# Output projection of a hybrid encoder block: 20 of 32 contraction tiles by one Strassen level

## The chip, the core and the metric

One NeuronCore of a Trainium2 chip runs the whole block in one launch. The metric is the device time of that launch in microseconds (us), and a time is given as the median of several runs. TensorE (PE in the rows, PEld for its weight loads) multiplies, VectorE (DVE) and ScalarE (ACT) work on elements, GpSimd (POOL) and SyncE (SP) mostly start DMA transfers.

## What is computed

The input x is 512 tokens by 4096 channels in float32. One layer:

```
h = rmsnorm(x) * pre_norm
z = h @ w_in            # 9808 columns: q, c, qi, kix, wix, gate_a, pool_in, gate_b
ya = sparse_attention(q, c, qi, kix, wix) * silu(gate_a)      # 2048 channels
yb = multiscale_pool(pool_in) @ w_pool * scale * silu(gate_b) # 2048 channels
y = concat(ya, yb) @ w_out                                    # 4096 x 4096
out = x + rmsnorm(y) * post_norm
```

The change concerns the product with `w_out`: 512 tokens, contraction over 4096 channels, 4096 output columns.

## The kernel before

Every float32 product is made of three matmuls on halves of the numbers: `split` (lines 57 to 59) casts a tile to a rounded type on ACT (the high half, `hi`) and subtracts it from the original on DVE (the low half, `lo`); `mm3` (lines 70 to 74) adds high x high, high x low and low x high in PSUM. `staged` (lines 61 to 68) loads a 128 x 512 weight tile of 256 KB through SP's DMA queue and splits it; its three buffers `raw`, `hi`, `lo` have four places each, so weights can be prepared four tiles ahead.

The channels are cut into 32 tiles of 128 (`NK`), the tokens into 4 blocks of 128 (`NB`). A first stage normalises x and keeps the halves `xh`, `xl` of all 32 tiles in SBUF, in 32 buffers of the pool `big`. Then `group` (lines 235 to 245) makes 128 columns of z at a time: 8 weight tiles, 32 x 3 matmuls into one bank of PSUM, an evacuation, and between the weight tiles one step of a background queue `bg` (lines 247 to 268) that spreads attention and pooling over the groups. The gated results, 32 tiles of 128 channels x 512 tokens, go to a DRAM tensor `cat` (`put`, line 334). The last groups are those of the fourth pool group (`pool_group`, lines 349 to 395, with g = 3), each followed by a gate.

The output projection follows (lines 481 to 557). `reload` brings tiles of `cat` back, splits them, and keeps the halves `ch`, `cl` in the buffers that `xh` and `xl` had. `chunk(db, blocks)` makes 512 output columns for the given token blocks: for each of the 32 contraction tiles one weight tile of `wout` and 12 matmuls of 512 columns (6 for two blocks). Its result is squared and summed on ACT and multiplied by the gain on DVE (lines 504 to 509). The column blocks 0 to 4 (`NFULL` = 5) take all four token blocks at once; blocks 5 to 7 take token blocks 0 and 1 first, so that `finish((0, 1))` can write half of the output while blocks 5 to 7 run again for tokens 2 and 3, with their weights loaded a second time. `finish((2, 3))` comes at the end: 16 multiply-adds on DVE, each followed by a store.

The code is traced; a scheduler then orders each engine's instructions, and each engine executes its own list in that order.

Of the kernel before, what the change touches and what calls it, by code (L numbers as in the profile page):

```python
# [43 lines left out]
def block_kernel(ctx: ExitStack, tc: tile.TileContext, xT, x, gk, wc, wkw, wf, wuk, wuv, kvn,  # L44
                 ikg, ikb, wpool, pscale, wout, gpost, ident_in, invc_in, out):
# [288 lines left out]
    def put(e, src, scl, sg):  # L334
        V.scalar_tensor_tensor(sg, src, scl, sg, op0=ALU.mult, op1=ALU.mult)
        if e == NK - 1:
            split(sg, *[t[:, 1] for t in cat_tile(NK // 2 - 1)])
        else:
            nc.sync.dma_start(cat[e], sg)

    ct = {}

    def cat_tile(i):
        if i not in ct:
            ct[i] = (big.tile([P, 2, S], F32R, tag=f"h{i}", name=f"ch{i}"),
                     big.tile([P, 2, S], F32R, tag=f"l{i}", name=f"cl{i}"))
        return ct[i]

    def pool_group(pl, g):
# [36 lines left out]
        for d in range(4):  # L386
            yp = bank()
            bg.add(ymix(d, yp), 1)

            def evac(z, d=d, yp=yp):  # L390
# [229 lines left out]
```

## Time and profile before

| what | value |
| --- | --- |
| median of 3 runs | 2624.4 us (2623.66 to 2629.9) |
| span of the profiled execution (no other time is listed for it) | 2626.6 us |
| TensorE busy, matmuls | 2587.6 us (99%), 11768 |
| DVE busy, ACT busy, POOL busy | 1176.9 us (45%), 863.8 us (33%), 46.7 us (2%) |
| DMA, mean over the span | 119 GB/s |
| loads of `wout` | 352 of 256 KB |

Matmuls are pipelined: the duration in a row runs from a matmul's start to its modelled end and overlaps the next ones. What a matmul costs in a stream is the distance between two starts. Idle time of an engine that is not the bottleneck costs nothing by itself.

### The profile page before, as it was taken

The page shows a single profiled execution, that of the slowest core. Times are in us where ns is not written, and L with a number is a line of the kernel's source. Part 1 is how long each engine was busy: PE and PEld are TensorE (multiplying, and loading weights), DVE is VectorE, ACT ScalarE, POOL GpSimd, SP SyncE. Part 2 cuts the span into 40 slices and gives each one's busy share as a digit, 9 for nine tenths or more (in the row PEclk, how much of TensorE's full clock was granted, in tenths as well). Part 3 has the DMA queues.
Part 4 walks back from the last instruction along what each step waited for, and adds up shares of the span by engine and source line. Part 5 has one row for each costly group of instructions (what it writes and reads, how often), then busy time and mean ns, then how long its engine had stood idle before and what let it go on. Part 6 is the DMA issues. An engine that isn't in the chain of part 4 may idle for free.

```text
span 2626.6 us, 31765 instructions
## 1 busy us (share of the span) xinstructions
PE 2587.6 (99%) x11768; PEld 2147.4 (82%) x11768; DVE 1176.9 (45%) x2086; ACT 863.8 (33%) x1542; POOL 46.7 (2%) x36
## 2 busy tenths in 40 slices
PE   7999999999999999999999999999999999999997
PEld 5799888888888888888888888888888888888875
DVE  9465783344344444444344334344452222235655
ACT  5344322233333333333332222222342222235443
POOL 5100000000000000000000000000000000000000
PEclk9999999999999999999999999999999999999998
DMA  6334333333333333333333333333473333346786
GB/s 202 99 100 109 96 100 107 103 92 90 98 94 92 89 97 92 92 93 92 94 93 97 106 106 96 105 104 101 129 224 101 101 97 103 101 133 197 224 284 220
DMA packets 169068, 312.15 MB, mean 119 GB/s; under 512 B 19536, under 2 KB 19664, under 8 KB 168912
## 3 DMA queue, kind: packets, MB, share of 16 engines
q1 hardware_dynamic: 168912, 310.12, 40.5%
q8 instruction: 92, 1.51, 0.2%
q14 instruction: 64, 0.52, 0.1%
HBM read 293.53 MB, written 16.52 MB: 118 GB/s over the span
## 4 chain that ended last, share of the span: by engine, by line
PE 90%; DMA 2%; DVE 1%; ACT 0%; issue 0%; DVEq 0%; SPq 0%; ACTq 0%
PE ps_acc L72 21%; PE ps_acc L74 20%; PE ps_acc L73 20%; PE ps_w L73 9%; PE ps_w L74 9%; PE ps_w L72 9%; DMA raw<-in_wout 2%; PE ps_w L447 1%; PE ps_w L279 1%; DVE lo L59 0%; DVE xr L530 0%; DMA xr<-in_x 0%; ACT hi L58 0%; DMA out<-xr 0%; DVE yg L509 0%
## 5 line engine op out<-in xcount | busy, mean ns | idle before, releaser
L59 DVE TENSOR_TENSOR lo<-raw,hi 128x512 fp32r<-128x512 f32 x1008 | 698.7, 695 | 1216.7 <-ACT hi L58 1143.2
L58 ACT CAST hi<-raw 128x512 fp32r<-128x512 f32 x1008 | 626.2, 622 | 1548.4 <-PE ps_acc L73 929.1
L72 PE MATMUL ps_acc<-xh,hi 128*128 128x512 f32 (+1 forms) x2304 | 893.0, 388 | 0.0
L74 PE MATMUL ps_acc<-xh,lo 128*128 128x512 f32 (+1 forms) x2304 | 883.9, 384 | 0.0
L73 PE MATMUL ps_acc<-xl,hi 128*128 128x512 f32 (+1 forms) x2304 | 883.7, 384 | 0.0
L72 PEld LDWEIGHTS ps_acc<-xh,hi 128*128 128x128 f32 x2304 | 432.7, 188 | 81.5 <-issue 2.2
L74 PEld LDWEIGHTS ps_acc<-xh,lo 128*128 128x128 f32 x2304 | 432.4, 188 | 81.4 <-issue 0.2
L73 PEld LDWEIGHTS ps_acc<-xl,hi 128*128 128x128 f32 x2304 | 433.0, 188 | 76.3
L73 PE MATMUL ps_w<-lo,ch 128*128 128x512 f32 x864 | 338.3, 392 | 3.3 <-DVE lo L59 3.2
L72 PE MATMUL ps_w<-hi,ch 128*128 128x512 f32 x864 | 337.2, 390 | 1.8 <-ACT hi L58 1.8
L74 PE MATMUL ps_w<-hi,cl 128*128 128x512 f32 x864 | 336.9, 390 | 0.0
L73 PEld LDWEIGHTS ps_w<-lo,ch 128*128 128x128 f32 x864 | 162.6, 188 | 41.8 <-DVE lo L59 8.3
L72 PEld LDWEIGHTS ps_w<-hi,ch 128*128 128x128 f32 x864 | 162.5, 188 | 36.7 <-ACT hi L58 2.7
L74 PEld LDWEIGHTS ps_w<-hi,cl 128*128 128x128 f32 x864 | 162.6, 188 | 33.4
L73 PE MATMUL ps_w<-lo,xh 128*128 128x512 f32 x128 | 52.9, 414 | 9.6 <-DVE lo L59 9.6
L72 PE MATMUL ps_acc<-hi,ch 128*128 128x512 f32 x160 | 62.2, 389 | 0.0
L73 PE MATMUL ps_acc<-lo,ch 128*128 128x512 f32 x160 | 62.2, 389 | 0.0
L74 PE MATMUL ps_acc<-hi,cl 128*128 128x512 f32 x160 | 62.2, 389 | 0.0
L72 PE MATMUL ps_w<-hi,xh 128*128 128x512 f32 x128 | 52.5, 410 | 7.1 <-ACT xh L58 6.4
L426 ACT ACTIVATE prob<-prob,nm 128x128 f32<-128x128 f32 (+1 forms) x64 | 36.1, 564 | 63.3 <-DVE nm L423 63.3
L74 PE MATMUL ps_w<-hi,xl 128*128 128x512 f32 x128 | 52.2, 408 | 0.0
L155 POOL TENSOR_TENSOR sumsq<-sumsq,sq 128x512 f32<-128x512 f32 x31 | 45.9, 1481 | 34.0 <-ACT sq L151 32.8
(180 smaller groups left out, 1601.3 us busy)
## 6 DMA issues: line engine op xcount, KB each, us to landing
raw<-in_wf SPq DMA_DIRECT2D x576, 256.0 KB, 2.6
raw<-in_wout SPq DMA_DIRECT2D x352, 256.0 KB, 2.9
raw<-in_wc SPq DMA_DIRECT2D x32, 256.0 KB, 2.7
xr<-in_x SPq DMA_DIRECT2D x32, 256.0 KB, 4.7
out<-xr SPq DMA_DIRECT2D x32, 256.0 KB, 2.3
cat_raw<-cat SPq DMA_DIRECT2D x31, 256.0 KB, 2.9
xt<-in_xT SPq DMA_DIRECT2D x15, 512.0 KB, 3.6
raw<-in_wpool SPq DMA_DIRECT2D x16, 256.0 KB, 2.6
```

Source lines behind the costliest of these rows:

```text
L58: A.copy(hi, src)
L59: V.tensor_sub(lo, src, hi.bitcast(F32))
L72: nc.tensor.matmul(dst, lh, rh, start=start, stop=False)
L73: nc.tensor.matmul(dst, lh, rl, start=False, stop=False)
L74: nc.tensor.matmul(dst, ll, rh, start=False, stop=stop)
L155: nc.gpsimd.tensor_add(sumsq, sumsq, sq)
L279: nc.tensor.matmul(dp[j][:, :n], lhs[j][x0], rhs[j][x1], start=i == 0, stop=i == 2)
L426: A.activation(pb, pb, AF.Exp, scale=-1.0, bias=nm, accum_out=sm)
L447: nc.tensor.transpose(tp[:, ts(b - s, P)], prob[:, OFF[b] + P * s:OFF[b] + P * s + P], ident)
```

## The change

The first 20 contraction tiles are taken in 10 pairs (tile i and tile i + 10, `KA` = 10). For a pair, tokens are cut in two halves of 256 and each block of 512 output columns in two halves of 256, which makes 2 x 2 blocks on each side, and one level of Strassen's scheme in the form with 15 additions needs 7 products instead of 8. `operands` builds the 7 token operands of a pair from `cat` once (4 additions, 7 splits); `weights` builds the 7 weight operands of a pair and column block (3 instructions, 7 splits) from one load of 512 KB out of `wq`, a copy of `w_out` in that order. In a step (db, i) each of the 7 products is two matmul triples of 256 columns into its own bank of PSUM; the sums run over the 10 pairs of a column block. After the tenth pair ACT copies the 7 banks to SBUF, DVE combines them (`collect`), and POOL's DMA queue stores the partial sums of the block to DRAM (`part`).

The other 12 tiles (`EB`) are multiplied as before, after all Strassen steps, in lanes; `NFULL` is now 6, so two column blocks are cut into half lanes. At the end of a lane the partial sum, loaded from `part`, is added to the result before it is squared. All 32 tiles of `cat` now go through DRAM.

`xh` and `xl` lie in ten larger buffers, so that operand tiles can take them one after the other. For that the last two gate groups run interleaved, one eighth of the contraction each in turn (`group` with a tuple), and one operand tile is made per eighth; the first is made during the gate group before, tiles 8 and 9 during the first Strassen steps.

```diff
-NFULL, XR = 5, 6
+NFULL = 6
+H = S // 2
+KA = 10
+EB = NK - 2 * KA
...
     def put(e, src, scl, sg):
         V.scalar_tensor_tensor(sg, src, scl, sg, op0=ALU.mult, op1=ALU.mult)
...
+        nc.sync.dma_start(cat[e], sg)
+
+    def operands(i, pool, tag, bufs, home):
+        w = pool.tile([P, 8, H], F32, tag=tag, name="cw", bufs=bufs)
+        q, s = w[:, 0:4], w[:, 4:8]
+        for j in range(2):
+            nc.sync.dma_start(q[:, 2 * j:2 * j + 2], cat[i + KA * j].rearrange("p (a t) -> p a t", a=2))
+        V.tensor_add(s[:, 0], q[:, 1], q[:, 3])
+        V.tensor_sub(s[:, 2], q[:, 0], q[:, 1])
+        V.tensor_sub(s[:, 1], s[:, 0], q[:, 0])
+        V.tensor_sub(s[:, 3], q[:, 2], s[:, 1])
+        yield
+        o = home([P, 2, 7, H], f"ops{i}")
+        split(w[:, 0:3:2], o[:, 0, 0:2], o[:, 1, 0:2])
+        split(w[:, 3:8], o[:, 0, 2:7], o[:, 1, 2:7])
...
+    def weights(db, i):
+        w = ow.tile([P, 8, H], F32, tag="wr", name="wr", bufs=2)
+        nc.sync.dma_start(w[:, 0:4], wq[i, db].rearrange("p (a c) -> p a c", a=4))
+        V.tensor_sub(w[:, 4:6], w[:, 1:3], w[:, 0:2])
+        V.tensor_sub(w[:, 6], w[:, 2], w[:, 4])
+        V.tensor_sub(w[:, 7], w[:, 3], w[:, 6])
+        hi = ow.tile([P, 7, H], F32R, tag="wh", name="wh", bufs=2)
+        lo = ow.tile([P, 7, H], F32R, tag="wl", name="wl", bufs=2)
+        split(w[:, 0:3:2], hi[:, 0:2], lo[:, 0:2])
+        split(w[:, 3:8], hi[:, 2:7], lo[:, 2:7])
+        return hi, lo
...
+            group((G_GB + 4 * g + 2, G_GB + 4 * g + 3), (evs[2], evs[3]), before=before, after=after)
...
+    PRODUCTS = ((0, 0), (1, 2), (4, 5), (5, 4), (3, 3), (2, 6), (6, 1))
+    def collect(db, pt):
+        V.tensor_add(pt[:, 1], pt[:, 0], pt[:, 1])
+        V.tensor_add(pt[:, 2], pt[:, 2], pt[:, 0])
+        yield
+        V.tensor_add(pt[:, 3], pt[:, 3], pt[:, 2])
+        V.tensor_add(pt[:, 0], pt[:, 3], pt[:, 4])
+        yield
+        V.tensor_add(pt[:, 4], pt[:, 4], pt[:, 2])
+        V.tensor_add(pt[:, 3:5], pt[:, 3:5], pt[:, 5:7])
+        yield
+        nc.gpsimd.dma_start(part[db, :, 0], pt[:, 1])
+        nc.gpsimd.dma_start(part[db, :, 3], pt[:, 0])
+        nc.gpsimd.dma_start(part[db, :, 1:3], pt[:, 3:5])
...
+    for n, (db, i) in enumerate(order):
+        if i == 0:
+            banks = [bank() for _ in range(6)] + [bank("acc")]
+        wh, wl = ready.pop(n)
+        o = ops[i]
+        for (a, w), z in zip(PRODUCTS, banks):
+            for h in range(2):
+                zz, ab = z[:, ts(h, H)], (o[:, 0, a, ts(h, P)], o[:, 1, a, ts(h, P)])
+                nc.tensor.matmul(zz, ab[0], wh[:, w], start=i == 0 and h == 0, stop=False)
+                nc.tensor.matmul(zz, ab[0], wl[:, w], start=False, stop=False)
+                nc.tensor.matmul(zz, ab[1], wh[:, w], start=False, stop=i == KA - 1 and h == 1)
+        if n + 2 < len(order):
+            ready[n + 2] = weights(*order[n + 2])
...
+        if i == KA - 1:
+            pt = oc.tile([P, 7, 512], F32, name="pt")
+            for j, z in enumerate(banks):
+                A.copy(pt[:, j], z)
+            bg.add(collect(db, pt))
+        bg.step()
...
+        for i, b in enumerate(blocks):
+            mm3(yp[i], tuple(t[:, ts(b, P)] for t in ct[e]), wo, e == 0, e == EB - 1)
+        if e == 3:
+            pg = opl.tile([P, 512], F32, name="pg", bufs=2)
+            nc.sync.dma_start(pg, gpost[:, ts(db, 512)].to_broadcast([P, 512]))
+            for b in blocks:
+                pp[b] = opl.tile([P, 512], F32, name="pp", bufs=6)
+                nc.sync.dma_start(pp[b].rearrange("p (a c) -> p a c", a=2),
+                                  part[db, :, b // 2::2, ts(b % 2, H)])
+        if e == EB - 1:
...
+            for i, b in enumerate(blocks):
+                V.tensor_add(pp[b], yp[i], pp[b])
+            for i, b in enumerate(blocks):
+                junk = opl.tile([P, 512], mybir.dt.bfloat16, name="junk")
+                A.activation(junk, pp[b], AF.Square, accum_out=yss[b][:, db:db + 1])
```

What the scheduler makes of it is shown at three places. Names with numbers are buffers; `wr`, `wh`, `wl` are a weight tile, its high and its low halves. In the changed kernel the split stands at lines 65 (cast) and 66 (low half), the three subtractions at 385 to 387, the copies of the banks at 637, `collect` at 577 to 584.

ACT at the end of a column block, before (squares of the four banks between the casts of weights two tiles ahead):

```order
L58 CAST hi_15977<-raw_15975 128x512
L506 ACTIVATE junk_15917,yss0_15177<-ps_w_15203 128x512
L506 ACTIVATE junk_15921,yss1_15178<-ps_w_15204 128x512
L506 ACTIVATE junk_15925,yss2_15179<-ps_w_15205 128x512
L506 ACTIVATE junk_15929,yss3_15180<-ps_acc_15206 128x512
L58 CAST hi_15995<-raw_15993 128x512
```

and now, at the end of the first column block (tile 10 is `wh_15791`, tile 11 `wh_15844`):

```order
L65 CAST wh_15791<-wr_15786 128x1280
L637 COPY pt_15850<-ps_w_15289 128x512
L637 COPY pt_15850<-ps_w_15290 128x512
L637 COPY pt_15850<-ps_w_15291 128x512
L637 COPY pt_15850<-ps_w_15292 128x512
L637 COPY pt_15850<-ps_w_15293 128x512
L637 COPY pt_15850<-ps_w_15294 128x512
L65 CAST wh_15844<-wr_15839 128x512
L65 CAST wh_15844<-wr_15839 128x1280
L637 COPY pt_15850<-ps_acc_15295 128x512
```

Six of the seven copies stand ahead of the casts of tile 11, although the code asks for these first; the seventh bank belongs to a pair of banks of its own.

DVE at the same place, before:

```order
L59 TENSOR_TENSOR lo_15978<-raw_15975,hi_15977 128x512
L509 TENSOR_TENSOR yg_15919<-ps_w_15203,pg_15201 128x512
L509 TENSOR_TENSOR yg_15923<-ps_w_15204,pg_15201 128x512
L509 TENSOR_TENSOR yg_15927<-ps_w_15205,pg_15201 128x512
L509 TENSOR_TENSOR yg_15931<-ps_acc_15206,pg_15201 128x512
L59 TENSOR_TENSOR lo_15996<-raw_15993,hi_15995 128x512
```

and now, from the long split of tile 11 to that of tile 12 (`wr_15909`), with the first subtractions of tile 13 (`wr_15964`):

```order
L66 TENSOR_TENSOR wl_15845<-wr_15839,wh_15844 128x1280
L385 TENSOR_TENSOR wr_15909<-wr_15909 128x512
L583 TENSOR_TENSOR pt_15850<-pt_15850 128x512
L386 TENSOR_TENSOR wr_15909<-wr_15909 128x256
L584 TENSOR_TENSOR pt_15850<-pt_15850 128x1024
L387 TENSOR_TENSOR wr_15909<-wr_15909 128x256
L66 TENSOR_TENSOR wl_15915<-wr_15909,wh_15914 128x512
L385 TENSOR_TENSOR wr_15964<-wr_15964 128x512
L386 TENSOR_TENSOR wr_15964<-wr_15964 128x256
L66 TENSOR_TENSOR wl_15915<-wr_15909,wh_15914 128x1280
```

Adds of `collect` and the subtractions of tile 13, which wait for that tile's load, stand ahead of the long split of tile 12. Away from the block's end the odd tile's first subtraction stands there too.

DVE around the last gate, before:

```order
L330 TENSOR_TENSOR gate_z_15163<-ps_acc_14999,R_72 128x512
L59 TENSOR_TENSOR lo_15284<-raw_15281,hi_15283 128x512
L59 TENSOR_TENSOR cl4_15302<-cat_raw_15299,ch4_15301 128x512
L332 SCALAR_TENSOR_TENSOR sg_15162<-sg_15162,gate_z_15163 128x512
L59 TENSOR_TENSOR cl4_15302<-cat_raw_15305,ch4_15301 128x512
```

and now (`ops7` is the operand tile of the seventh pair after the first, `wr_15247` and `wr_15258` are weight tiles 0 and 1):

```order
L66 TENSOR_TENSOR ops7_15230<-cw_15205,ops7_15230 128x512
L385 TENSOR_TENSOR wr_15247<-wr_15247 128x512
L66 TENSOR_TENSOR ops7_15230<-cw_15205,ops7_15230 128x1280
L386 TENSOR_TENSOR wr_15247<-wr_15247 128x256
L66 TENSOR_TENSOR wl_15253<-wr_15247,wh_15252 128x512
L387 TENSOR_TENSOR wr_15247<-wr_15247 128x256
L356 TENSOR_TENSOR gate_z_15270<-ps_acc_14873,R_76 128x512
L66 TENSOR_TENSOR wl_15253<-wr_15247,wh_15252 128x1280
L385 TENSOR_TENSOR wr_15258<-wr_15258 128x512
L66 TENSOR_TENSOR wl_15264<-wr_15258,wh_15263 128x512
L386 TENSOR_TENSOR wr_15258<-wr_15258 128x256
L358 SCALAR_TENSOR_TENSOR sg_15269<-sg_15269,gate_z_15270 128x512
```

Before, tiles of `cat` and of `wout` were split ahead of and around the last gate; now the first two weight tiles stand behind the last operand tile, and the gates between their splits.

## Rows read from the trace of the kernel before

**Rows 1.** The page: engines, and the chain that ended last, by engine.
```profile
PE 2587.6 (99%) x11768; PEld 2147.4 (82%) x11768; DVE 1176.9 (45%) x2086; ACT 863.8 (33%) x1542; POOL 46.7 (2%) x36
...
PE 90%; DMA 2%; DVE 1%; ACT 0%; issue 0%; DVEq 0%; SPq 0%; ACTq 0%
```
**Rows 2.** Stretches: us; busy PE, PEld, DVE, ACT, POOL; clock, DMA share, GB/s.
```profile
300.00:400.00 100.00, 100.00 (x443) 82.77 (x442) 82.36 (x214) 25.17 (x42) 0.00 (x0) 1.00 0.36 98
1400.00:1500.00 100.00, 100.00 (x442) 82.50 (x441) 36.37 (x59) 25.54 (x41) 0.00 (x0) 1.00 0.35 103
2480.00:2580.00 100.00, 94.92 (x394) 73.81 (x393) 57.05 (x87) 43.30 (x74) 0.00 (x0) 0.98 0.88 284
```
**Rows 3.** Timeline of TensorE, first and last of 39 matmuls: start us, duration us.
```profile
1429.83 0.39 PE L72 MATMUL ps_acc<-xh,hi 128*128 128x512 f32 x1
...
1438.45 0.39 PE L74 MATMUL ps_acc<-xh,lo 128*128 128x512 f32 x1
```
**Rows 4.** Timeline, three matmuls of 256 columns in attention and the next one.
```profile
1011.32 0.28 PE L72 MATMUL ps_w<-kh,qh 128*128 128x256 f32 x1
...
1011.43 0.28 PE L73 MATMUL ps_w<-kl,qh 128*128 128x256 f32 x1
1011.43 0.19 PEld L74 LDWEIGHTS ps_w<-kh,ql 128*128 128x128 f32 x1
...
1011.67 0.40 PE L72 MATMUL ps_acc<-xh,hi 128*128 128x512 f32 x1
```
**Rows 5.** Timeline of TensorE, the last of three matmuls of 128 columns, and its successor.
```profile
1008.42 0.27 PE L74 MATMUL ps_w<-kh,ql 128*128 128x128 f32 x1
1008.53 0.44 PE L72 MATMUL ps_acc<-xh,hi 128*128 128x512 f32 x1
```
**Rows 6.** Groups of TensorE in the projection; each stands for three lines (72 to 74).
```profile
L72 PE MATMUL ps_w<-hi,ch 128*128 128x512 f32 x864 | 337.2, 390 | 1.8 <-ACT hi L58 1.8
...
L72 PE MATMUL ps_acc<-hi,ch 128*128 128x512 f32 x160 | 62.2, 389 | 0.0
```
**Rows 7.** Timeline of TensorE, first and last matmul of the projection.
```profile
1902.45 0.39 PE L72 MATMUL ps_w<-hi,ch 128*128 128x512 f32 x1
...
2609.55 0.39 PE L74 MATMUL ps_w<-hi,cl 128*128 128x512 f32 x1
```
**Rows 8.** Groups of DVE by shape: count, busy us, mean ns, idle us before.
```profile
L59 DVE TENSOR_TENSOR lo<-raw,hi 128x512 fp32r<-128x512 f32 x1008 | 698.7, 695 | 1216.7 <-ACT hi L58 1143.2 <-PE ps_w L447 34.6 <-PE ps_w L73 33.5
...
L59 DVE TENSOR_TENSOR xl<-gx,xh 128x512 fp32r<-128x512 f32 x32 | 26.7, 854 | 1.5 <-ACT xh L58 1.5
...
L59 DVE TENSOR_TENSOR kwl<-kwr,kwh 128x640 fp32r<-128x640 f32 x4 | 3.3, 814 | 0.0
...
L229 DVE TENSOR_TENSOR kd<-kt,ib 128x256 f32<-128x256 f32 x2 | 0.8, 424 | 0.1
```
**Rows 9.** Timeline of DVE, two neighbours without a gap.
```profile
320.68 0.68 DVE L59 TENSOR_TENSOR lo<-raw,hi 128x512 fp32r<-128x512 f32 x1
321.28 0.70 DVE L361 TENSOR_TENSOR ws<-pu 128x527 f32<-128x527 f32 x1
```
**Rows 10.** Groups of ACT by shape.
```profile
L58 ACT CAST hi<-raw 128x512 fp32r<-128x512 f32 x1008 | 626.2, 622 | 1548.4 <-PE ps_acc L73 929.1 <-PE ps_acc L74 278.3 <-issue 89.0
...
L58 ACT CAST kwh<-kwr 128x640 fp32r<-128x640 f32 x4 | 2.9, 722 | 0.0
```
**Rows 11.** DMA issues of the first stage: count, KB each, us to landing.
```profile
xt<-in_xT SPq DMA_DIRECT2D x15, 512.0 KB, 3.6
...
kwr<-in_wkw SPq DMA_DIRECT2D x4, 320.0 KB, 4.9
```
**Rows 12.** Waits in 2470:2610: who waited for whom, us, times, longest.
```profile
ACT hi L58 <- DMA raw<-in_wout: 47.3, 37, 5.7
```
**Rows 13.** Timeline after the last matmul: ACT's last square, DVE's last multiply-adds.
```profile
2610.03 0.60 ACT L506 ACTIVATE junk<-ps_w 128x512 bf16<-128x512 f32 x1
...
2613.48 10.02 DVE L530 SCALAR_TENSOR_TENSOR xr<-yg,ry,xr 128x512 f32<-128x512 f32 x15
```

More of the change, by code (lines that the diff above doesn't have):

```diff
@@ L335, in put, with pool_group @@
         V.scalar_tensor_tensor(sg, src, scl, sg, op0=ALU.mult, op1=ALU.mult)
[L336 to L349, printed above, removed]
+        nc.sync.dma_start(cat[e], sg)
+    ops = {}
+    def operands(i, pool, tag, bufs, home):
[11 more added lines that the diff above has]
+        split(w[:, 3:8], o[:, 0, 2:7], o[:, 1, 2:7])
+        ops[i] = o
+        yield
[10 more added lines that the diff above has]
+        return hi, lo
+    order = [(db, i) for db in range(8) for i in range(KA)]
+    ready = {}
+    def pool_group(pl, pm, g):
         w = WINS[g]
@@ L384, in ymix, with gated, evac @@
                 yield
[L386 to L390, printed above, removed]
+        def gated(d, yp):
+            def evac(z):
                 bg.drain(1)
@@ L394, in evac, with add, rest, early @@
                 put(16 + 4 * g + d, yp, psc[:, 4 * g + d:4 * g + d + 1], sg)
-            group(G_GB + 4 * g + d, evac, 2 if d == 0 else 1)
+            return evac
+        def add(d):
+            yp = bank()
+            bg.add(ymix(d, yp), 1)
+            return gated(d, yp)
+        if g < 3:
+            for d in range(4):
+                group(G_GB + 4 * g + d, add(d), 2 if d == 0 else 1)
+            return lambda: None
+        evs = [add(d) for d in range(4)]
+        group(G_GB + 4 * g, evs[0], 2)
+        bg.drain(1)
+        def rest():
+            first = []
+            def early(q):
+                if q == 3:
+                    first.append(operands(0, ow, "wr", 2, lambda sh, n: ex.tile(sh, F32R, name=n)))
+                if q in (3, 5):
+                    next(first[0])
+            group(G_GB + 4 * g + 1, evs[1], after=early)
+            cur = []
+            def before(q, i):
+                if i == 0:
+                    cur[:] = [operands(q, ow, "wr", 2, lambda sh, n: big(q - 1, sh, n))] if q else []
+                for e in cur:
+                    next(e)
+            def after(q):
+                if q == 7:
+                    for n in range(2):
+                        ready[n] = weights(*order[n])
+            group((G_GB + 4 * g + 2, G_GB + 4 * g + 3), (evs[2], evs[3]), before=before, after=after)
+        return rest
     V.tensor_scalar(psc, psc, 0.5, None, op0=ALU.mult)
-    with tc.tile_pool(name="pl0", bufs=1, reuse_waits="tile") as pl:
-        pool_group(pl, 0)
+    with tc.tile_pool(name="pl0", bufs=1, reuse_waits="tile") as pl, \
+            tc.tile_pool(name="pm0", bufs=1, reuse_waits="tile") as pm:
+        pool_group(pl, pm, 0)
         bg.drain()
@@ new lines, in block_kernel, with load_cat, prefetch @@
+    lanes = [(db, (0, 1, 2, 3)) for db in range(NFULL)]
+    lanes += [(db, p) for p in ((0, 1), (2, 3)) for db in range(NFULL, 8)]
+    steps = [(n, e) for n in range(len(lanes)) for e in range(EB)]
+    ahead, ct, late = {}, {}, []
+    def load_cat(e):
+        raw = st.tile([P, S], F32, tag="raw", name="cat_raw")
+        nc.sync.dma_start(raw, cat[2 * KA + e])
+        ct[e] = (fin.tile([P, S], F32R, name=f"ch{e}"), fin.tile([P, S], F32R, name=f"cl{e}"))
+        split(raw, *ct[e])
+    def prefetch(n):
+        if n < len(steps) and n not in ahead:
+            lane, e = steps[n]
+            if n < EB:
+                load_cat(e)
+            ahead[n] = staged(wout[lanes[lane][0], e])
```

217 lines of the change are left out of this document (126 added, 91 removed).

## Prediction, on record before the change was run

> **What bounds the kernel now.** First the page's engine line and its chain that ended last [rows 1]: TensorE is busy for 99% of the span and holds 90% of the chain; no other engine holds over 1%, DMA 2%. So the end moves by what TensorE streams, plus what it waits. Second, the stages [rows 2]: about 442 matmuls per 100 us at full clock, also in 300:400, where DVE is 82% busy; busy neighbours do not slow TensorE. The exception is 2480:2580, where 394 matmuls stand for 443 and DMA has its highest share, 0.88 at 284 GB/s. Third, what one matmul costs: the durations in the groups overlap, so I take spacings of starts. 512 columns: 38 matmuls in 8.62 us [rows 3], 0.2268 us each. 256 columns: a run of three in 0.35 us [rows 4], 0.117 each.
>
> Half a wide matmul would be 0.1134. The rest is a fixed cost: 512 columns at 2.4 GHz are 0.2133, leaving 0.0135 per matmul; 256 columns are 0.1067, and with the same 0.0135 that gives 0.120. I take 0.120, the larger. A weight load starts with the matmul before it and lasts 0.19 [rows 4], but 128-column matmuls, each with its load, follow each other at 0.11 [rows 5], so loads overlap in part and can be issued every 0.11: just under 0.120.
>
> The Trainium skill ("TensorE: Matmul & The Clock Gate", Back-to-back issue gap) gives N/2.4 + 2.5 ns, so 0.109 and 0.216; by it the products below would gain 47 us, not 32. The trace disagrees (0.117 and 0.2268), and the measurement decides.
>
> **The products.** The projection runs 3 x 864 + 3 x 160 = 3072 matmuls [rows 6] of 512 columns, 696.7 us at 0.2268. It lasts from 1902.45 to 2609.55 + 0.23 [rows 7], 707.3 us; 10.6 are lost, nearly all in 2480:2580: 49 matmuls missing there are 11.1 us [rows 2].
> After: 80 Strassen steps (8 column blocks x 10 tile pairs) of 7 products x 2 halves x 3 = 42 matmuls of 256 columns: 3360 x 0.120 = 403.2 us, one step 5.04. The 12 direct tiles: 8 x 12 x 4 x 3 = 1152 x 0.2268 = 261.3. Sum 664.5, **32.2 less**. Seven eighths of the columns would give 54 for the 20 tiles; the fixed cost on twice as many instructions takes back 22.
> Before the last pool group TensorE keeps its order.
>
> **Feeding a Strassen step.** One step needs a 512 KB load, three subtractions (512, 256, 256 columns) and two splits (512 and 1280). DVE: 512 columns start 0.60 apart [rows 9]; durations are 0.424 for 256, 0.695 for 512, 0.814 for 640 [rows 8], about 1.02 ns a column, so 1280 last 1.46 (an estimate). With the 0.09 by which neighbours overlap: 0.61 + 0.34 + 0.34 + 0.61 + 1.39 = 3.3 of 5.04 us. ACT: 0.62 and, from 0.622 and 0.722 [rows 10], 1.22 for 1280: 1.8 us. Throughput suffices; what counts is the loop. With two buffers a load starts when the low half of the tile two before is done, and by the DVE order the subtraction of the odd tile stands ahead of the even tile's long split. Around two steps: load 3.6 (the 512 KB of the first stage [rows 11]), subtraction 0.61, long split 1.39, two subtractions 0.34 + 0.42, long cast 1.22, long split 1.46, some 0.1 of signals: 9.1 of 10.08 us. So TensorE is not held in the steady state, with 1.0 us per pair to spare.
>
> **Block boundaries.** Seven evacuations to SBUF on ACT and seven adds on DVE (6 x 0.61 + 1.13 = 4.8 us) per block. In the ACT order six evacuations stand ahead of the next cast and each follows its product by 0.72 us, so banks are free in time. On DVE the adds delay the splits: counted from the start of a block's last step along the order rows, the long split of the block's third-next tile ends at 15.5, and TensorE wants it at 3 x 5.04 + 0.84 = 15.96. That fits by 0.4, but a load 1 us later (4.9 was seen [rows 11]) makes it 1.6 late. I take 0.4 each, 3 us for 7 boundaries; ends 0 and 12. The stores go through POOL, idle there today; nothing waits for them until the direct part. No row prices them; where POOL worked, in the first stage, a 512-column split took 0.854 instead of 0.695 [rows 8]; that is inside the 12.
>
> **Start.** While the last two gate groups run interleaved, DVE has per eighth 2 x 0.61 + 4 x 0.34 + 0.61 + 1.39 = 4.6 of TensorE's 24 x 0.2268 = 5.44 us, and four weight buffers lie ahead: no loss there. But the last operand tile's buffer comes free only at the end of the seventh eighth, its split stands in DVE's order ahead of the first two weight tiles, and between those stand two gates. Adding along those rows, the first tile's long split ends 2.3 us after the last gate matmul and is wanted at 0.84: 1.5 lost; the next tiles, their loads waiting for buffers and DVE making up operands 8 and 9 as well, lose 1.0, 1.0, 0.9 and 0.5. **5 us**, ends 0 and 12. SP's cat stores stand ahead of the fourth weight load, but that one waits for its buffer longer.
>
> **Last lanes.** The split into half lanes now covers 2 blocks x 12 tiles instead of 3 x 32, so the reloading of weights at double rate shrinks from 192 steps to 48. It is heaviest in the last two lanes: 24 weight tiles, 16 outputs, four partial sums and two gains, 46 x 0.262 = 12.1 MB in 32.7 us, 369 GB/s; 284 at a share of 0.88 [rows 2] means 323 at most, so 37.3 us: 4.6 lost. DVE has 24 x 0.61 + 16 x 0.67 [rows 13] + about 6 = 31 there, just enough. Before, waits of casts for these weights add up to 47.3 us [rows 12], of which TensorE felt 11. **4.5 us**, ends 0 and 10. After the last matmul an add precedes the square, which today follows it by 0.25 us [rows 13]: 0.5 more, ends 0 and 1.5.
>
> **The sum.** -32.2 products, -10.6 old losses, + 5 + 3 + 4.5 new losses, + 0.5 = **-29.8 us** against the profiled execution. No time is listed for it beside its span, 2626.6, 2.2 above the median of the three runs and inside their range. 2624.4 - 29.8 gives **2594 us**. All low ends, and 0.117 for a matmul, give -53; all high ends -7.
>
> **The rivals.**
> *The loop of a weight pair is longer than two steps* and TensorE waits in all 40 pairs. It decides from 10.08 us on; from 10.85 it has eaten the 30 us, and beyond that the kernel is slower. With the load at 4.9 [rows 11] and DVE's four long terms longer by 0.854/0.695 it is 9.1 + 1.3 + 0.8 = 11.2: 40 x 1.1 = 45 us more, **2639**. For it: one buffer ahead only, and DVE waits in line for the load. Against: the 4.9 fell in the loaded first stage, while the Strassen stage moves 512 KB per 5.04 us, 104 GB/s. Chance 0.12, half of it beyond break-even.
> *Weight loads bind.* If the 0.19 of a load could not overlap the next, 3360 x 0.188 = 632 us, 228 more: **2822**. Or, if a load could not overlap the matmul before it, 0.107 + 0.11 = 0.217 against 0.213 + 0.11 = 0.323: 3360 x 0.217 against 1920 x 0.323 is 729 against 620, 109 more than those tiles cost today under that rule, **2733**. The rows speak against both: 512 columns come every 0.2268, not 0.323, and loads every 0.11 [rows 3 to 5]; what is not shown is a long run of such matmuls. Chance 0.04. The second is a rule of the Trainium skill (same page, What overlaps and what doesn't: a load overlaps running matmuls only for another row group); the trace disagrees.
> *The ends cost more*: start and last lanes at 12 and 10 instead of 5 and 4.5, about **2607**. For it: in 2480:2580 the same traffic cost 11 us. Chance 0.14.
> *The forecast*: 0.70.
>
> **The numbers.** Within 0.3% (8 us, about what a measurement of this kernel can tell from none) lies 2616.5 to 2632.3. Faster: forecast 0.69, ends 0.13, a mild loop 0.02, 0.84 together; same: 0.01 + 0.01 + 0.05 of the loop = 0.07; slower: 0.05 of the loop and the weight loads, 0.09. The range 2578 to 2616 takes in the forecast's bounds but for the farthest low ones, and the costlier ends.
>
> **What would show it.** Right: 256-column matmuls 0.117 to 0.121 apart in the middle of a column block, projection about 677 us, TensorE idle 1 us or less at block boundaries and some 5 at its start. Wrong: spacings of 0.13 or more; waits for the low halves in every other step; idle time before the first product of a block waiting for the evacuations; a granted clock at its lower level in the projection.

## The result, and the profile after

The changed kernel takes **2601.71 us** (median of 4 runs, 2600.48 to 2602.74) beside 2625.93 for the kernel before on the same chip: ratio 0.9904, 95% interval 0.9892 to 0.9916, so 24 us faster. The forecast was 2594, with a range of 2578 to 2616. The profiled executions span 2600.1 us after and 2626.6 before: 26.5 less, where the prediction's sum was 29.8.

The page, engines and chain by engine, as [rows 1]:

```profile
PE 2555.0 (98%) x13208; PEld 2190.8 (84%) x13208; DVE 1368.3 (53%) x2374; ACT 898.1 (35%) x1526; POOL 60.0 (2%) x60
...
PE 87%; DVE 3%; DMA 2%; ACT 1%; issue 0%; DVEq 0%; ACTq 0%
```

TensorE still holds the chain, with 1440 more matmuls and 33 us less busy time. DVE holds 3% of the chain instead of 1%. The projection by stretches, columns as in [rows 2]: start, middle and end of the Strassen part, the six full lanes, half lanes 6 and 7, half lanes 8 and 9, the tail:

```profile
1902.20:1922.00 19.80, 19.08 (x153) 18.38 (x152) 18.61 (x30) 8.70 (x11) 0.00 (x0) 1.00 0.52 160
1922.00:2262.00 340.00, 338.05 (x2813) 337.35 (x2812) 267.56 (x381) 147.71 (x185) 10.40 (x19) 1.00 0.39 124
2262.00:2310.80 48.80, 48.09 (x401) 47.88 (x401) 39.05 (x57) 22.77 (x31) 1.08 (x2) 1.00 0.56 184
2310.80:2506.70 195.90, 195.90 (x867) 162.19 (x866) 81.12 (x126) 63.34 (x124) 1.62 (x3) 1.00 0.58 193
2506.70:2542.20 35.50, 33.21 (x146) 26.86 (x145) 20.90 (x34) 18.02 (x36) 0.00 (x0) 1.00 0.70 226
2542.20:2582.80 40.60, 35.79 (x145) 27.62 (x143) 31.21 (x62) 16.97 (x32) 0.00 (x0) 0.96 0.71 236
2582.80:2600.10 17.30, 0.13 (x1) 0.00 (x0) 14.04 (x34) 1.74 (x6) 0.00 (x0) 0.58 0.63 243
```

The full lanes have no gap at all. What TensorE loses lies in the Strassen part (0.7, 2.0 and 0.7 us without a running matmul in the first three rows) and, mostly, in the half lanes, where 32.7 us of matmuls take 35.5 and 40.6. To compare kernels I count a loss in a piece as the distance from its first matmul to the next piece's first, less its matmuls at 0.120 us (256 columns) or 0.2267 (512). "Start" is the first column block, "boundaries" the other seven blocks; spans are of the profiled execution, and losses are good to 0.1 us. The first row adds up: 403.2 + 261.2 + 2.5 + 3.0 + 10.9 makes 680.8, and from 1902.19 to the last matmul's end at 2582.77 it is 680.6.

| kernel | start | boundaries | lane 0 | lanes 6, 7 | lane 8 | lane 9 | span |
| --- | --- | --- | --- | --- | --- | --- | --- |
| changed | 2.5 | 3.0 | 0.0 | 2.9 | 4.4 | 3.5 | 2600.1 |
| changed, again (e9) | 2.2 | 3.1 | 0.0 | 3.7 | 3.8 | 3.5 | 2598.5 |
| e3 output late | 2.4 | 4.0 | 0.0 | 5.2 | 0.0 | 1.6 | 2597.0 |
| e4 2 KB rows | 3.3 | 3.4 | 0.1 | 3.7 | 2.9 | 3.4 | 2599.8 |
| e5 sums by POOL | 2.9 | 4.2 | 4.1 | 4.9 | 3.6 | 2.7 | 2604.4 |
| e6 adds spread | 3.2 | 5.7 | 0.0 | 5.9 | 3.8 | 3.0 | 2604.0 |
| e7 e3 + e5 | 3.6 | 3.6 | 4.5 | 2.5 | 0.7 | 2.7 | 2599.3 |
| e10 own buffers | 3.5 | 3.9 | 0.5 | 1.3 | 0.2 | 3.7 | 2596.4 |
| e12 e10, stores by POOL | 3.0 | 2.7 | 2.1 | 1.3 | 0.0 | 4.0 | 2596.9 |

The same code gives up to 1 us more or less in a column from one execution to the next (the first two rows). The boundaries, where DVE's list is the same in all nine rows, range from 2.7 to 5.7 (more on that below). Nine entries hold about 1.5 us of TensorE's lower clock (granted clock 0.50) behind a wait: lane 8 in the first two rows, lanes 6 and 7 in e3, e4, e5 and e6, the boundaries in e6, lane 0 in e7 and lane 9 in e10. To compare waits, take that off first. Where the loss comes from is read at two places. Lane 8, first DVE, then TensorE:

```profile
2549.45 4.73 DVE L674 SCALAR_TENSOR_TENSOR sp<-yg,ry,sp 128x512 f32<-128x512 f32 x7
2554.09 0.68 DVE L66 TENSOR_TENSOR lo<-raw,hi 128x512 fp32r<-128x512 f32 x1
```

```profile
2551.71 0.61 PE L79 MATMUL ps_w<-hi,ch 128*128 128x512 f32 x2
2554.83 0.69 PE L80 MATMUL ps_w<-lo,ch 128*128 128x512 f32 x1 [2.51 <-DVE lo L66]
2555.32 0.63 PE L81 MATMUL ps_w<-hi,cl 128*128 128x512 f32 x1
2555.75 0.63 PE L80 MATMUL ps_w<-lo,ch 128*128 128x512 f32 x1
```

Seven multiply-adds of the first output half stand in a row ahead of the low half that TensorE needs. After the wait of 2.5 us the next starts are 0.43 apart, which is 512 columns at 1.2 GHz; eight such spacings cost 1.6 us more than 0.2267 each; the granted clock is 0.50 there (2555.00:2558.40). So a wait can be paid again in the clock, but need not be. At the entry to lane 6 the changed kernel run again (e9) waited longer, and the granted clock stayed at 1.00 (2516:2520):

```profile
2517.14 0.49 PE L79 MATMUL ps_w<-hi,ch 128*128 128x512 f32 x1 [2.64 <-ACT hi L65]
```

That entry to lane 6 is the second place. SP's queue in the changed kernel:

```profile
2505.51 0.33 SPq L71 DMA_DIRECT2D raw<-in_wout  x1
2508.55 1.83 SPq L695 DMA_DIRECT2D pp<-part  x3
2510.44 0.59 SPq L692 DMA_DIRECT2D pg<-in_gpost  x1
2511.12 2.44 SPq L71 DMA_DIRECT2D raw<-in_wout  x4
```

For 5.6 us no weight load is issued; then four go out behind three partial sums and a gain.

### The profile page after: what moved, and what is told of

Same layout as the page of the kernel before. It is cut to its first block, busy times and chain, and to the rows that moved or that the text cites. A ratio compares the mean times of both kernels' runs of the same rounds, so it can differ in the third digit from the quotient of the medians.

```text
span 2600.1 us, 34361 instructions
## 1 busy us (share of the span) xinstructions
PE 2555.0 (98%) x13208; PEld 2190.8 (84%) x13208; DVE 1368.3 (53%) x2374; ACT 898.1 (35%) x1526; POOL 60.0 (2%) x60
## 4 chain that ended last, share of the span: by engine, by line
PE 87%; DVE 3%; DMA 2%; ACT 1%; issue 0%; DVEq 0%; ACTq 0%
PE ps_acc L79 20%; PE ps_acc L81 20%; PE ps_acc L80 20%; PE ps_w L80 5%; PE ps_w L81 5%; PE ps_w L79 5%; PE ps_w L619 4%; PE ps_w L618 4%; PE ps_w L617 4%; DMA wr<-in_wq 1%; DVE wl L66 1%; PE ps_w L533 1%; PE ps_w L305 1%; PE ps_acc L619 1%; PE ps_acc L617 1%; PE ps_acc L618 1%
## 5 line engine op out<-in xcount | busy, mean ns | idle before, releaser
L79 PE MATMUL ps_acc<-xk,hi 128*128 128x512 f32 (+1 forms) x2304 | 893.1, 388 | 0.0
L81 PE MATMUL ps_acc<-xk,lo 128*128 128x512 f32 (+1 forms) x2304 | 884.0, 384 | 0.0
L80 PE MATMUL ps_acc<-xk,hi 128*128 128x512 f32 (+1 forms) x2304 | 883.7, 384 | 0.0
L79 PEld LDWEIGHTS ps_acc<-xk,hi 128*128 128x128 f32 x2304 | 432.7, 188 | 81.3 <-issue 2.2
L81 PEld LDWEIGHTS ps_acc<-xk,lo 128*128 128x128 f32 x2304 | 432.4, 188 | 81.5 <-issue 0.2
L80 PEld LDWEIGHTS ps_acc<-xk,hi 128*128 128x128 f32 x2304 | 433.0, 188 | 76.2
L618 PE MATMUL ps_w<-wl,ops 128*128 128x256 f32 x960 | 270.2, 282 | 2.9 <-DVE wl L66 2.8
L619 PE MATMUL ps_w<-wh,ops 128*128 128x256 f32 x960 | 270.6, 283 | 0.0
L617 PE MATMUL ps_w<-wh,ops 128*128 128x256 f32 x960 | 269.0, 282 | 0.5 <-DVE sg L361 0.5
L617 PEld LDWEIGHTS ps_w<-wh,ops 128*128 128x128 f32 x960 | 179.9, 188 | 0.7 <-DVE sg L361 0.7
L619 PEld LDWEIGHTS ps_w<-wh,ops 128*128 128x128 f32 x960 | 180.5, 188 | 0.0
L80 PE MATMUL ps_w<-lo,ch 128*128 128x512 f32 x312 | 122.8, 394 | 5.0 <-DVE lo L66 4.9
L79 PE MATMUL ps_w<-hi,ch 128*128 128x512 f32 x312 | 120.7, 391 | 2.1 <-ACT hi L65 2.1
L81 PE MATMUL ps_w<-hi,cl 128*128 128x512 f32 x312 | 122.2, 392 | 0.0
```

The lines of the kernel that those rows point to most:

```text
L79: nc.tensor.matmul(dst, lh, rh, start=start, stop=False)
L80: nc.tensor.matmul(dst, lh, rl, start=False, stop=False)
L81: nc.tensor.matmul(dst, ll, rh, start=False, stop=stop)
L617: nc.tensor.matmul(zz, ab[0], wh[:, w], start=i == 0 and h == 0, stop=False)
L618: nc.tensor.matmul(zz, ab[0], wl[:, w], start=False, stop=False)
L619: nc.tensor.matmul(zz, ab[1], wh[:, w], start=False, stop=i == KA - 1 and h == 1)
```

## The experiments

**A fixed cost per matmul?** e1, in the direct part:

```diff
-            mm3(yp[i], tuple(t[:, ts(b, P)] for t in ct[e]), wo, ...)
+            for c in range(2):
+                nc.tensor.matmul(yp[i][:, ts(c, H)], lh, rh[:, ts(c, H)], ...)
...
```

> The 1152 direct matmuls of 512 columns are cut into 2304 of 256 columns; weights, loads and the Strassen part stay. Theory (a fixed 0.0135 us per matmul beside its columns): starts 0.120 apart also with these other operands, in a direct lane without waits, so 276.5 us streamed for 261.3, +15 us, less up to 4 of the last lanes' waits, which have more time: +11 to +15. Rival (no fixed cost, the 0.120 belongs to the Strassen operands or their feeding): 0.1134 apart, 0 to +1 us. Rival (weight loads bind once every matmul has 256 columns and its own load): 0.19 apart, +170 us.

Ratio 0.9946 (0.993 to 0.9963); span 2613.9, 13.8 more. First and last of 25 starts in a direct lane:

```profile
2400.07 0.28 PE L692 MATMUL ps_w<-hi,ch 128*128 128x256 f32 x1
...
2402.95 0.28 PE L692 MATMUL ps_w<-hi,ch 128*128 128x256 f32 x1
```

2.88 us / 24 = 0.120, with other operands than the Strassen part's. The fixed cost of 0.0135 per matmul holds (N/2.4 GHz is 0.1067 and 0.2133, the rows show 0.120 and 0.2267), and with it what the prediction took back from the saved columns. By the formula of the Trainium skill ("TensorE: Matmul & The Clock Gate", Back-to-back issue gap: N/2.4 + 2.5 ns, called there the gap of an isolated matmul) the cut would cost 3 us, an estimate; the run disagrees.

**How near is the loop of a weight pair to its limit?** The first subtraction of each weight tile is repeated, in e2 three more times, in e8 once (`range(2)`):

```diff
-        V.tensor_sub(w[:, 4:6], w[:, 1:3], w[:, 0:2])
+        for _ in range(4):
+            V.tensor_sub(w[:, 4:6], w[:, 1:3], w[:, 0:2])
```

> The first subtraction of every weight tile (512 columns on DVE, 0.61 us) is made four times over, with the same result: 1.83 us more DVE work per step. Theory (the loop of a pair of tiles through two buffers, 9.1 us of 10.08, holds one of these subtractions): 9.1 + 1.8 = 10.9, so in the middle of a column block two steps take 10.8 to 11.0 us, with the waits in every other step; 40 x 0.85 = 34 us, and 10 to 30 more because the adds of a boundary find no free time: +40 to +65 us. Rival (only DVE's throughput counts, 3.3 + 1.83 = 5.13 per step against 5.04): two steps take 10.26, 7 us plus the adds of seven boundaries, +10 to +40. Rival (the loop is much shorter than 9 us and DVE's time is not all needed): two steps stay at 10.08, under +10 us.

> The first subtraction of a weight tile is made twice, 0.72 us more DVE work per step with its neighbour's wait, 1.44 for a pair of tiles. Four times over (4.3 us more for a pair) a pair took 12.3 us. Theory (the loop of a pair is 9.1 us and holds one of the two tiles' subtractions): 9.8, two steps stay at 10.08 in mid block; only the boundaries grow, +3 to +10 us. Rival (the loop holds both tiles' subtractions, so 12.3 - 4.3 = 8.0 is what it lasts in the changed kernel): 9.4, two steps stay at 10.08 too, +2 to +8. Rival (the loop already lasts 10.08 to 10.1, just hidden): two steps take 10.8 to 11.5, +30 to +55 us.

e2: ratio 1.0332 (1.0316 to 1.0347), span 2710.4, +110 us: in mid block two steps mostly take 12.1 to 12.5 us. e8: ratio 1.0053 (1.004 to 1.0066), span 2637.3, +37 us: two steps take 10.4 to 10.7 in the middle of most blocks, and up to 12.0 in others. Both are above what my theory gave, and e8's total is that of its last rival. DVE's rows tell why. The changed kernel, from a short low half on:

```profile
2184.72 0.69 DVE L66 TENSOR_TENSOR wl<-wr,wh 128x512 fp32r<-128x512 f32 x1 [0.86 <-ACT wh L65]
2185.78 0.69 DVE L385 TENSOR_TENSOR wr<-wr 128x512 f32<-128x512 f32 x1 [0.37 <-DMA wr<-in_wq]
2186.39 1.49 DVE L66 TENSOR_TENSOR wl<-wr,wh 128x1280 fp32r<-128x1280 f32 x1
...
2188.25 0.43 DVE L387 TENSOR_TENSOR wr<-wr 128x256 f32<-128x256 f32 x1
```

and e8 (its lines stand one further down):

```profile
2204.26 0.69 DVE L386 TENSOR_TENSOR wr<-wr 128x512 f32<-128x512 f32 x1
2204.86 0.69 DVE L66 TENSOR_TENSOR wl<-wr,wh 128x512 fp32r<-128x512 f32 x1
2205.46 0.69 DVE L386 TENSOR_TENSOR wr<-wr 128x512 f32<-128x512 f32 x1
...
2206.64 0.42 DVE L388 TENSOR_TENSOR wr<-wr 128x256 f32<-128x256 f32 x1
```

With the longer list DVE's order is another: the short low half now stands between a tile's first subtraction and its last ones, inside the chain. 9.1 + 0.72 + 0.61 = 10.4, and 10.66 was measured. ACT's casts now wait for the last subtraction (e8, 2150:2250: us, times, longest):

```profile
ACT wh L65 <- DVE wr L388: 50.1, 16, 3.4
```

In the changed kernel the last subtraction ends at 2188.68, while ACT's two casts run from 2189.11 to 2190.90, so the long one (1.26) begins at 2189.64, held by the short one, which waits for TensorE's last use of the buffer:

```profile
2189.11 1.79 ACT L65 CAST wh<-wr 128x512 fp32r<-128x512 f32 x2 [3.25 <-PE ps_acc L619]
```

That is a reserve of 0.85 us with a signal's 0.1, near the 1.0 predicted. But the reserve belongs to that order of instructions: one subtraction more per tile used it up and made the kernel slower than the one before.

**Boundaries.** e6 puts one add of `collect` into each step:

```diff
         V.tensor_add(pt[:, 1], pt[:, 0], pt[:, 1])
+        yield
         V.tensor_add(pt[:, 2], pt[:, 2], pt[:, 0])
         yield
...
```

> The seven adds that combine a column block's products (DVE, 4.8 us) are spread over seven Strassen steps, one in each, instead of two in each of three. Theory (two adds of 0.61 in one step push the low halves of the block's third-next tile past the time at which TensorE wants them: 1.84, 0.87 and 0.1 us lost there): these waits fall under 0.5 in sum; -2 to -3 us. Rival (a load landing late, or the copies of the banks on ACT, cause them): they stay at 1 to 3 us.

Ratio 0.9915 (0.9902 to 0.9927): not better, boundaries 5.7 (4.2 without the clock's share). DVE's order around them is the changed kernel's, row for row: the scheduler puts the adds into the same gaps wherever the program has them, so this run decides nothing on spreading. What it does show, with the others, is the load. At the first boundary of the changed kernel, DVE and then TensorE:

```profile
1965.19 0.69 DVE L385 TENSOR_TENSOR wr<-wr 128x512 f32<-128x512 f32 x1 [1.26 <-DMA wr<-in_wq]
...
1966.25 1.48 DVE L66 TENSOR_TENSOR wl<-wr,wh 128x1280 fp32r<-128x1280 f32 x1
```

```profile
1965.83 0.28 PE L617 MATMUL ps_w<-wh,ops 128*128 128x256 f32 x1
1967.79 0.39 PE L618 MATMUL ps_w<-wl,ops 128*128 128x256 f32 x1 [1.68 <-DVE wl L66]
```

The load for the row at 1965.19 was issued at 1960.35 and took 4.82 us; the block lost 1.9. In e5 the same load took 4.28, in e1 5.13, in e6 5.46, and the block lost 1.1, 3.7 and 3.75. Of the last two 1.5 each is the lower clock behind the wait (granted clock 0.50 in 1964.9:1968.1 of e1 and 1968.5:1971.8 of e6), so the waits are 1.1, 1.9, 2.2 and 2.3 us, in the order of the loads; the other runs follow that only roughly (4.50 went with 1.0 in e12, 4.45 with 1.95 in e7). At the five boundaries in between such a load takes about 3.6 and 0 to 0.5 is lost; at the last 0.9 to 2.4, where loads 71 and 74 were late. Of the 80 loads those with the numbers 7, 10, 13, 71, 74 and 79 took 4.1 to 6.0 us in each of the ten kernels of which DVE's Strassen list is the changed kernel's (median of all 80 there: 3.6), so it isn't chance. The traces show what ran beside them: in these ten kernels every load over 4.0 us has a packet of the instruction queues (q8 and q14 on the page) in flight, but for numbers 9 and 79, beside which 0.4 MB of other data or more moved. Yet only 86 of the 303 loads with such a packet took over 4.0 us, and no run tried it: the cause is open.

e11 takes the adds off DVE, on top of e10 below: `nc.gpsimd.tensor_add` for the six `V.tensor_add` of a block.

> The run before plus the adds that combine a block's products on POOL instead of DVE. Theory (these adds put the load and the long split of a block's second and third tile behind, and TensorE waits where that load lands 1 us late as well): block boundaries lose under 0.7 in sum instead of 1.1 to 4; 1 to 3 us less than the run before. Rival (POOL's adds, on the same memory, slow DVE: in the first stage a 512-column split took 0.854 instead of 0.695): splits within the adds' time last over 0.75, boundaries lose 3 us or more, time above that of the run before. Rival (the late loads alone cause the waits): boundaries unchanged, 1 to 4.

Ratio 0.9997 (0.9988 to 1.0006), span 2624.1: all of the gain is gone. The boundaries and the start lose 33 us. DVE beside POOL's adds:

```profile
2065.12 1.52 DVE L386 TENSOR_TENSOR wr<-wr 128x256 f32<-128x256 f32 x1
2066.67 1.40 DVE L387 TENSOR_TENSOR wr<-wr 128x256 f32<-128x256 f32 x1
```

```profile
2064.07 2.28 POOL L577 TENSOR_TENSOR pt<-pt 128x512 f32<-128x512 f32 x1 [41.85 <-ACT pt L637]
2066.32 1.47 POOL L578 TENSOR_TENSOR pt<-pt 128x512 f32<-128x512 f32 x1
```

A 256-column subtraction lasts 1.52 us there and 0.42 without; the rival was right, and its price of 0.854 against 0.695 far too low. The Trainium skill ("SBUF — State Buffer", Terms: the port pair of the two engines is held for a whole instruction and the other engine is blocked) fits: DVE's 256-column row is longer by 1.1 us, less than one of POOL's adds (1.47, 2.28). A later pair shows it best; the subtraction starts 0.06 us after an add of POOL and ends 0.30 after it:

```profile
2074.42 2.65 DVE L386 TENSOR_TENSOR wr<-wr 128x256 f32<-128x256 f32 x1
```

```profile
2074.36 2.41 POOL L584 TENSOR_TENSOR pt<-pt 128x1024 f32<-128x1024 f32 x1
```

**The last lanes.** e3 takes the first half of the output out of the lanes:

```diff
-            if lane == NFULL + 8 - NFULL:
-                bg.add(finish((0, 1)))
...
-    for _ in finish((2, 3)):
-        pass
+    for p in ((0, 1), (2, 3)):
+        for _ in finish(p):
+            pass
```

> The first half of the output (16 multiply-adds on DVE and 16 stores) is taken out of the last lanes and made after the last matmul, ahead of the second half. The time after the last matmul grows by 10.7 (16 x 0.667 on DVE) to 13 us (4.2 MB at 323 GB/s). Theory (these multiply-adds and stores make the last two lanes lose 7.9 us): the last two lanes lose under 1.5, so the kernel is +3 to +6 us. Rival (the weights loaded at double rate and the partial sums make the loss): lanes still lose 6 to 8, +10 to +13 us. In both, the 2.9 of the first half lane after the six full ones stays.

Ratio 0.9887 (0.9872 to 0.9902), span 2597.0, 3.1 less. Lanes 8 and 9 lose 1.6 instead of 7.9 (6.3 without the clock's share), as the theory said. But both expectations had 10.7 us or more added after the last matmul, and that time did not grow (17.9 against 17.4). Later in the program only means lower rank for the scheduler, which fills DVE's gaps with these multiply-adds, one between two low halves:

```profile
2554.67 0.74 DVE L674 SCALAR_TENSOR_TENSOR sp<-yg,ry,sp 128x512 f32<-128x512 f32 x1
2555.34 0.68 DVE L66 TENSOR_TENSOR lo<-raw,hi 128x512 fp32r<-128x512 f32 x1
...
2556.01 0.74 DVE L674 SCALAR_TENSOR_TENSOR sp<-yg,ry,sp 128x512 f32<-128x512 f32 x1
```

For lane 6 there were four runs. e4 stores `part` by token block:

```diff
-                nc.sync.dma_start(pp[b].rearrange("p (a c) -> p a c", a=2),
-                                  part[db, :, b // 2::2, ts(b % 2, H)])
+                nc.sync.dma_start(pp[b], part[db, b])
```

> The partial sums lie in DRAM by token block, so that a load takes rows of 2 KB where it took pieces of 1 KB; the stores, in the Strassen part, now go in pieces of 1 KB. Same bytes. Theory (the small pieces make these loads slow, and the weight loads behind them in lane 6 land in 6.5 us): the lane loses under 1 instead of 2.9, and lane 9 a little less; -2 to -3 us. Rival (only the bytes ahead of the weight loads count): lane 6 still loses 2.5 to 3.2, the time within 1 us of the changed kernel. If the stores' smaller pieces disturb the Strassen part, its matmuls take over 409 us.

(This run also exchanges two of the four quarters of the partial sums, so its output is wrong; the bytes are the same.) Ratio 0.9901 (0.9886 to 0.9916); lanes 6 and 7 lose 3.7, without the clock's share 2.2 beside 2.9 and 3.7 in the first two rows: the size of the pieces is not the main thing. e5 and e7 (which is e3 and e5 together) change the queue of the partial sums and of the gain:

```diff
-                nc.sync.dma_start(pp[b].rearrange(...
+                nc.gpsimd.dma_start(pp[b].rearrange(...
```

> The loads of the partial sums and of the gain (pp, pg) in the direct part go through POOL's queue instead of SP's; same bytes, same places in the program. Theory (SP executes its queue in order: at the end of lane 5 it waits 2.6 us for a buffer of pp, with the weight loads of lane 6 behind, which then land late): lane 6 loses under 1 instead of 2.9, lanes 8 and 9 keep 6 to 8; -2 to -3 us. Rival (the bytes of four partial sums and a gain, 1.25 MB in 5 us beside the weights, make the loads slow, from whichever queue): lane 6 loses 2.5 to 5, the time within 1 us of the changed kernel. If POOL's issuing disturbs DVE, splits in lane 6 last over 0.75 us and it loses more.

> Both of: the first half of the output placed late in the program (lanes 8 and 9 lose 1.6 instead of 7.9) and pp, pg through POOL's queue (if SP's wait is the cause, lane 6 loses under 1). If the two add up: direct lanes lose under 2.5 in all where the changed kernel loses 10.8, 2592 us of span against 2600. If one gives back what the other gains (lane 6 lost 4.9 with the first alone), 2595 to 2598.

e5: 0.9928 (0.9915 to 0.9941), span 2604.4; e7: 0.9909 (0.9896 to 0.9922), 2599.3. SP's wait is not the cause either: lanes 6 and 7 lose 4.9 in e5 (3.4 without the clock's share), where POOL waits. And lane 0 now loses 4, so that e7 lies above both of its cases. Loads in 2311:2335, the changed kernel and then e5:

```profile
sp<-in_x SPq DMA_DIRECT2D x8, 256.0 KB, 5.7
raw<-in_wout SPq DMA_DIRECT2D x7, 256.0 KB, 3.6
```

```profile
sp<-in_x SPq DMA_DIRECT2D x12, 256.0 KB, 6.2
pp<-part POOLq DMA_DIRECT2D x6, 256.0 KB, 8.8
raw<-in_wout SPq DMA_DIRECT2D x4, 256.0 KB, 7.1
```

SP, no longer busy with partial sums, brings tiles of x forward that nothing needs for 200 us, and the weights beside them take 7.1 us instead of 3.6. That these tiles are what slows them was not tried by itself. e10 goes back to e3, leaves the full lanes' loads on SP and gives the half lanes' sums two buffers of their own, loaded, with the gain, through POOL:

```diff
+            tag, n_, queue = ("pp", 6, nc.sync) if lane < NFULL else ("ph", 2, nc.gpsimd)
...
-                pp[b] = opl.tile([P, 512], F32, name="pp", bufs=6)
-                nc.sync.dma_start(pp[b].rearrange(...
+                pp[b] = opl.tile([P, 512], F32, tag=tag, name="pp", bufs=n_)
+                queue.dma_start(pp[b].rearrange(...
```

> The first half of the output late in the program, and in the half lanes the partial sums have two buffers of their own and come, with the gain, through POOL's queue; full lanes load them through SP as before. Theory (at the end of lane 5 four partial sums and a gain are released at once and go out beside four weight loads, 2.4 MB in some 6.5 us; with buffers of their own those of lane 6 are there long before): the weight loads of lane 6 land in under 4 us and lane 6 and 7 together lose under 1.5 instead of 5.1 (with the output late alone); lane 0 loses nothing, as SP's list is as before there; span 2592 to 2594. Rival (DVE's eight lane-end operations, 5 us without a low half, hold the raw buffers, and the burst of weight loads alone is late enough): lanes 6 and 7 still lose 3 to 5, span 2596 to 2598.

Ratio 0.9891 (0.9877 to 0.9904). Lanes 6 and 7 lose 1.3 (in e12 too) instead of the 2.9 to 3.7 that the first three rows lose without the clock's share, so the burst at the end of lane 5 was the larger part of the cause. The expected 4 us of landing was missed; what is left in lane 6:

```profile
raw<-in_wout SPq DMA_DIRECT2D x4, 256.0 KB, 5.3
pg<-in_gpost POOLq DMA_DIRECT2D x1, 256.0 KB, 5.2
```

Only the gain is beside these weights now. The span, expected at 2592 to 2594, is 2596.4, just 0.6 below e3's: start, lane 0 and lane 9 lose more than there. In 2311:2335, at lane 0, two of lane 6's partial sums now land (two of `pp` through POOL, median 7.6 us; in e12 9.0, and lane 0 loses 2.1). In lane 9 SP still waits 6.5 us in all for multiply-adds, which e12 removes by sending those 16 stores through POOL (`nc.gpsimd.dma_start(out[b, db], t)`):

> As the run with two own buffers for the half lanes' partial sums, and the 16 stores of the first half of the output go through POOL's queue; the second half's 16 stores stay on SP. Adds stay on DVE. Theory (in the last two lanes SP waits 6.5 us in ten waits for these multiply-adds, with the weight loads behind): weight loads of lane 9 are issued as their buffers come free, lane 9 loses under 1.5 instead of 3.7; the clock stays up there; the run is 2 to 3.5 us below that run's 2596.4 of span, 2593 to 2594.5. Rival (the stores' bytes beside the loads, and the four lane-end operations on DVE, are enough for the loss): lane 9 loses 2.5 to 4, the time within 1 us. If POOL's issuing holds DVE up, multiply-adds take over 0.8 us and lanes 8 and 9 lose more.

Ratio 0.9895 (0.9878 to 0.9911), span 2596.9: the rival. Lane 9 keeps its full clock, but its waits grow from 2.2 to 4.0. Loads in 2553:2563 of e10 and of e12:

```profile
raw<-in_wout SPq DMA_DIRECT2D x6, 256.0 KB, 4.1
```

```profile
out<-sp POOLq DMA_DIRECT2D x7, 256.0 KB, 6.0
raw<-in_wout SPq DMA_DIRECT2D x5, 256.0 KB, 6.1
```

What SP does not wait for, the weights meet on the DMA engines. Last, the yardstick on the chip of e10 and e11:

> The changed kernel once more, beside the next two on the same chip, so that differences of a few us can be read. All theories: ratio 0.988 to 0.993, direct lanes lose 9 to 12 us, again in lanes 6, 8 and 9; block boundaries 1 to 4.5, at the weight tiles whose loads land late.

0.9912 (0.9898 to 0.9925), losses in the table. Beside it e10 is 5 us faster in the medians (2598.50 against 2603.47) and 2 in the spans. e3, e10 and e12 are the fastest kernels here, by 2 to 5 us, with intervals that overlap the changed kernel's; between these three nothing is decided.

## Why the prediction was right

- **Products, -32.2.** Right: 0.120 in the middle of a block, 408.6 us for the Strassen part including its losses, and e1 shows that the fixed cost is the matmul's.
- **Weight loads bind (rival).** Excluded: 3360 matmuls, each with a load, 0.120 apart.
- **The loop, 9.1 of 10.08.** It held in mid block: steps are 5.04. The rival was nearer than its 0.12 said: e8 is what it looks like, 37 us for 0.7 us of DVE work per tile.
- **Start, 5.** Measured 2.5, and only in part where the working put it. The first tile's long split cost 0.5 instead of 1.5, the next four tiles 0.5 instead of 3.4. Another 0.7 is a wait that the working did not have, for a bank of PSUM that `put` (L361) was still reading:

```profile
1906.52 0.39 PE L617 MATMUL ps_w<-wh,ops 128*128 128x256 f32 x1 [0.48 <-DVE sg L361]
```

The last 0.8 lies at the seventh and the ninth tile, by the mechanism of the boundaries (the loads behind them took 5.4 and 4.2). The interleaved gate groups cost nothing: the first Strassen matmul starts at 1902.19, and the projection began at 1902.45 before.

- **Boundaries, 3.** Measured 3.0, by the mechanism named (the third-next tile's long split behind the next tile's subtraction, late when the load is 1 us late), but in two boundaries of seven, not 0.4 in each; that the sum fits is luck. The working's numbers have two slips: by its own 15.5 and 15.96 a load 1 us later makes the split 0.5 late, not 1.6, and a block has six adds (5 x 0.61 + 1.13 = 4.2 us), not seven.
- **Last lanes, 4.5.** This is the step that failed. It was priced as bytes over bandwidth in the last two lanes, 12.1 MB at 323 GB/s. Measured were 10.9, as much as before the change, at a mean DMA share of 0.71 and 236 GB/s in the last two lanes; and 323 GB/s is no ceiling, for e5 moved 360 in 2311:2335. It was order more than bytes. Seven multiply-adds in a row in lane 8 (e3 takes 6.3 of the 7.9 us away with the same bytes), a burst of partial sums at the entry to lane 6, which the term did not cover at all (e10), and the clock after one of the waits. Bytes remain in lane 9, where e12 took SP's waits away and gained nothing. "Just enough" for DVE over 32.7 us said nothing about who stands ahead of whom.
- **After the last matmul, +0.5.** 17.4 us against 16.8.

So -32.2 - 10.6 + 2.5 + 3.0 + 10.9 + 0.6 = -25.8, against 26.5 in the spans (0.3 of the rest is the earlier start). The start's 2.5 too much hides part of the lanes' 6.4 too little. Of the 7.1 us between 2594.6 and 2601.7, 3.3 are these terms (29.8 against 26.5). Most of the rest is that a difference of spans was taken off a median. A run's time is 1.8 us longer than its span (2601.91 and 2600.1 for the profiled one after), so the profiled execution before took about 2628.4 (an estimate), 4.0 above the 2624.4; the one after lay 0.2 above its median. 3.3 + 4.0 - 0.2 = 7.1.

## What to carry to other kernels

Price an arithmetic saving with the fixed cost per instruction measured in the trace: here seven eighths of the columns in 1.75 times as many matmuls gave 32 us, not 54. A stage whose engines have enough throughput still waits where one engine does several things in a row ahead of what the bottleneck needs; look for such rows, and move the batch late in the program so that it fills gaps. And when a queue is relieved, ask what it will now bring forward.

## What was not expected of the hardware

- POOL's elementwise adds stretched DVE's subtractions by up to 2.2 us each (0.42 to 2.65), enough to lose 28 us.
- A wait of 2.5 us on TensorE was followed by eight spacings at the lower clock level (0.43), also where the wait was 1.8 (e10, lane 9, granted clock 0.50 in 2564.2:2567.4), but not where it was 2.6 (e9, lane 6, granted clock 1.00). How long the wait is does not decide it alone.
- The load of the gain, one row of 2 KB to 128 partitions, takes 4.4 us in e10 with a single weight load beside it, which takes 4.6 there and 2.6 in the rest of the lane:

```profile
pg<-in_gpost POOLq DMA_DIRECT2D x1, 256.0 KB, 4.4
raw<-in_wout SPq DMA_DIRECT2D x1, 256.0 KB, 4.6
```

That the gain slows the weights was not tried by itself; loading it once in full, ahead of the lanes, would tell.
